# Low parts of the two raw weight quarters by a negative on ScalarE and an adding DMA

## The chip, the cores and the metric

The kernel runs on one core of one Trainium2 chip. The metric is the device time of one execution in microseconds (us), the median of three runs. The core has TensorE (PE), VectorE (DVE), ScalarE (ACT) and GpSimd (POOL), and SyncE (SP) and others issue DMAs. Each engine works through its own instructions in order; semaphores tie them together.

## The reference, cut to what matters

Two transformer blocks run one after the other on 512 tokens of width 1024, all in float32. The part that matters here are products of a token matrix and a weight of 1024 rows: two gates of the first block's mixer and the two feed-forward layers of width 2816.

```python
mix = jax.nn.sigmoid(g_conv) * y_conv + jax.nn.sigmoid(g_attn) * y_attn
h = h + mix @ w_o[l]
n = rmsnorm(h, g_ffn[l])
h = h + (jax.nn.silu(n @ w_gate[l]) * (n @ w_up[l])) @ w_down[l]
```

The second block ends in the same form of feed-forward layer. `g_conv` and `g_attn` are columns of `n @ w_in`.

## The kernel before, in words

A float32 product is made of three products of float32r parts: every operand is split into a high part (a rounded copy, by ACT) and a low part (the operand less its high part, by DVE), and `mm3` (lines 325 to 328) adds high*high, high*low and low*high in one PSUM bank. The third of them, line 328, is the first that reads the weight's low part.

Most columns of the two gates and of the gate and up weights go through `winograd` (line 410): two weight columns at a time, one unit, as seven products of quarters in the place of eight. There are 46 units: 8 in the mixer's gates (from 470 to 565 us of the span), 19 in the first feed-forward layer (650 to 830 us) and 19 in the second (1413 to 1600 us). A unit's weight comes in by one load of 1024 KB on SP (line 397) as four quarters 01, 00, 10, 11 in a tile `raw`. `quarters` (line 392) then makes seven operands in four calls of `parts`, and I call the four pairs of tiles A, B, C and D after their order:

- A: the quarters 01 and 00 as they are (`raw[:, :2]`), 24 matmuls;
- B: the sum of 10 and 11, put in the place of 10 by line 402, and 11 itself, 24 matmuls;
- C: two differences that POOL makes (lines 404 and 405), 24 matmuls;
- D: one difference that DVE makes (line 401), 12 matmuls.

A product of quarters has 4 pairs of tiles times three matmuls of 256 columns, so a unit is 84 matmuls. Each of A to D takes a tile `wh` and a tile `wl`, and there are three buffers of each. So A of the next unit takes the buffers of B of this unit, and D takes those of A: a cast can begin only when PE has read the older tile to its end.

The order of instructions on each engine is fixed when the program is built: a scheduler places them by its own estimate of when each can start. The mixer's gates have more work on POOL and DVE between the units: the sigmoid on ACT, the product with it on POOL (line 651, two to a unit), a sum and a split on DVE.

Of the kernel before, what the change touches and what calls it, by code (L numbers as in the profile page):

```python
# [10 lines left out]
F32 = mybir.dt.float32  # L11
# [3 lines left out]
AF = mybir.ActivationFunctionType  # L15
ALU = mybir.AluOpType
# [10 lines left out]
# wo units begun before the last k-tiles of mix are there  # L27
EARLY = 3
# convolution units emitted after each attention head
FILL = [1, 0, 0, 0, 0, 0, 0, 1, 0, 0, 0, 1, 2, 2, 2, 2]  # L30
# the hidden units by the plain product (tile, part); the others by winograd()
# [9 lines left out]
def cut12(x):  # L41
    """x in parts of 12 bits and a rest."""
    out = []
    for _ in range(3):
        e = 2.0 ** (math.floor(math.log2(x)) - 11)
        out.append(math.floor(x / e) * e)
        x -= out[-1]
    return out + [x]


class Stream:
    """Weights as units of [128, n]; the program's order of loads sets their order in memory."""
# [12 lines left out]
    def quarters(self, name, w):  # L65
        """Two columns of tiles by quarters, [row of the product, half of the sum]: 01, 00, 10, 11."""
        k = w.shape[0] // P
        t = w.reshape(2, k // 2, P, 2, P).transpose(2, 3, 0, 1, 4)
        self.add(name, np.stack([t[:, i, j] for i, j in ((0, 1), (0, 0), (1, 0), (1, 1))], 1))
# [32 lines left out]
def layout(i):  # L102
    """The program's inputs: permuted, tiled and joined copies of the arrays."""
# [78 lines left out]
    # rows of the outputs by the latent attention, the recurrence and the memory  # L182
# [23 lines left out]
    t = np.arange(P)  # L206
# [19 lines left out]
class Ring:  # L226
    """Slots that tiles of one role take in turn."""
# [14 lines left out]
class Kernel:  # L242
# [87 lines left out]
    def lin(self, w, x, out=None, first=True, last=True, k0=0):  # L330
        """out[m, t] += sum over k of w[k, m] x[k, t], w a loaded unit."""
        if out is None:
            out = self.ps("mm", 3)
        k = w[0].shape[1]
        for j in range(k):
            self.mm3(out, (w[0][:, j], w[1][:, j]), x[k0 + j], first and j == 0, last and j == k - 1)
        return out
# [9 lines left out]
    def parts(self, raw):  # L347
        """Quarters of a weight, [128, q, n], or sums of them, in two parts."""
        q, n = raw.shape[1:]
        w = [self.wp.tile([P, q * n], F32R, tag=t, bufs=3, name=self.name(t)) for t in ("wh", "wl")]  # L350
        w = [a.rearrange("p (q n) -> p q n", q=q) for a in w]
        self.split(*w, raw)
        return [[a[:, j].rearrange("p (k c) -> p k c", c=P) for a in w] for j in range(q)]

    def product(self, out, w, x, part, first=True, last=True):
        """out += w^T x[part], x by pairs of tiles as in halves()."""
        for k, (h, l) in enumerate(x):
            self.mm3(
                out, [a[:, k] for a in w], (h[:, part], l[:, part]), first and k == 0, last and k == len(x) - 1
            )  # L360

    def halves(self, src, rb, gain, out, done=None):
        """The right-hand operand src * gain * rb of winograd(): by pairs of a tile of each half of the sum,
        the parts 00, 10, 11, T1, T2, T3, -T4 of [128, 256] (indices: half of the sum, half of the tokens)."""
# [27 lines left out]
    def quarters(self, name):  # L392
        """A weight by quarters for winograd(): 01, 00, S1, 11, S4, S2, S3 as operands."""
# [6 lines left out]
        w = self.parts(raw[:, :2])  # L400
# [9 lines left out]
    def winograd(self, w, x, out):  # L410
        """A product of [2 tiles, 512] by seven products of quarters for eight (Winograd's form of Strassen's).
        out: the two rows of tiles, [128, 512] in SBUF."""
# [4 lines left out]
        # (00, 01) and (10, 11) of the result  # L417
# [21 lines left out]
    def bank(self):  # L439
        """A PSUM bank in two halves, the six of the tags in turn."""  # L440
        self.banks += 1
        ps = self.ps(*(("mm", 3), ("S", 2), ("mm", 3), ("S", 2), ("mm", 3), ("o", 1))[self.banks % 6])
        return ps.rearrange("p (a b) -> p a b", a=2)

    def operand(self, n, k, big=True):
        """Tiles for the two parts of a [k * 128, 512] matrix: list of (high, low)."""
# [13 lines left out]
    def square_sum(self, acc, src, first, scale=1.0, last=False):  # L460
        """acc += (src * scale)^2"""
# [10 lines left out]
    def sums(self, accs):  # L472
        """Sums over the partitions, tokens on the partitions: [128, tokens / 128] in PSUM."""
# [11 lines left out]
    def rstd(self, sums, dim, pre=None, post=1.0):  # L485
        """pre / sqrt(pre^2 sums / dim + eps) * post; shapes [128, ...] alike."""
# [15 lines left out]
        # a first value within 4% by the bits as an integer, then Newton's steps  # L502
# [10 lines left out]
    def bcast(self, r):  # L513
        """A per-token column, [128, n], as rows on every partition: [128, n * 128] in SBUF."""
# [8 lines left out]
    def start(self):  # L523
        """The first operand, and three units by row along with it."""
# [27 lines left out]
    def block1(self):  # L552
# [110 lines left out]
        # the operand's last tiles come late: the first products begin with the others  # L663
# [38 lines left out]
    def keys_steps(self, g, n, rb):  # L702
        """Keys of group g and queries of its four heads; the last step yields them."""
# [25 lines left out]
    def conv(self, n, rb, out):  # L729
        """The short convolution's gated outputs, one unit a step."""  # L730
# [21 lines left out]
    def nsa_cmp(self, g, qg, kc, kcz, gbr):  # L752
        """The compressed branch's weights for four heads, by key: rows 32 hh + key."""
        nc = self.nc
        mm = nc.tensor.matmul
        # scores by key, each head's keys in rows of their own, then by query
# [39 lines left out]
    def nsa_soft(self, h, q, kg, gbr):  # L796
        """The two causal branches' weights of a head, by query, times their gates."""
# [30 lines left out]
    def nsa_out(self, h, pt, pc, vc, V, o32):  # L828
        """The weights by key: transposed, split, then times the values."""
# [28 lines left out]
    def blocks(self, n, rb, first, out):  # L858
        """Overlapping blocks of keys and values: [128 = (half, feature), 16 places, 4 heads x 32 blocks]."""
# [22 lines left out]
    def compress(self, blocks):  # L882
        """Hidden units of the compressed keys and values in four steps, then the products into (kc, vc)."""
# [23 lines left out]
        # the values' hidden units four times over  # L907
# [14 lines left out]
        # values: rows 32 hh + block, zero but for the head hh of a group  # L922
# [15 lines left out]
    def ffn(self, pre, x, gain, n, nhold, acc, done, half=None):  # L938
        """w_down^T (silu(y w_gate) * (y w_up)), y = x * gain normed; n: x * gain as an operand; acc: its
        squares' sums; done(t, sum) takes each finished tile."""  # L940
# [53 lines left out]
        # the hidden units as an operand; the first four take the weights' tiles  # L994
# [25 lines left out]
    def tables(self):  # L1020
        """Rotation by position, times the gains: out = x * one + swapped x * two."""
# [6 lines left out]
        # five [128, 4, 32] temporaries  # L1028
# [42 lines left out]
    def rotate(self, out, x, one, two, tmp):  # L1071
        """x, one, two: [128, n, 64]; out [128, n, 2, 64], twice the same."""
# [10 lines left out]
    def hgrn(self, n, rb, rt, fill):  # L1083
        """Gated linear recurrence, as one causal [512, 512] matrix per head.

        A pair (s, t), s < t, belongs to the level m (a power of two) at which s lies in the lower and t
        in the upper half of one block of 2 m tokens; its decay is the product of the gates after s in
        the lower half (B) and of those up to t in the upper half (A)."""
        nc, c = self.nc, self.c
        # the gates' lower bound: a softmax over two rows of logits  # L1090
# [25 lines left out]
        # by head: k times B, then q times A  # L1116
# [5 lines left out]
        def diagonal(h):  # L1122
            """The pairs s == t."""
# [32 lines left out]
    def hgrn_level(self, m, h, z, fs, last=False):  # L1156
        """One level's factors, split: k times B of the lower halves and q times A of the upper; then the
        next level's, by the halves' total decays."""
# [5 lines left out]
        if not last:  # L1164
            # a block's total is at its first token
# [53 lines left out]
    def mem_operand(self):  # L1219
        """The memory as an operand without its per-token scale; the sum of its squares."""  # L1220
# [13 lines left out]
    def mem_kv(self, ops, hold, r, rb, kk, vv):  # L1234
        """The memory's keys and values, unit by unit."""
# [33 lines left out]
    def mem_soft(self, h, q, f, kk):  # L1269
        """A head's weights by query; f: the queries' scale, [128, 4]."""  # L1270
# [39 lines left out]
    def mla_kv(self, ckv, rt, sckv, krs, kn, kp, vh, vl):  # L1310
        """Keys and values by token; the keys normed but for the gain, their rotary part twice. Two steps
        of products and four of norms."""
# [21 lines left out]
        # the shared rotary part  # L1334
# [8 lines left out]
        # (sckv k_nope, rt k_rope) over their joint norm  # L1343
# [24 lines left out]
    def mla_q(self, cq, scq):  # L1368
        """Queries by token, a block of tokens a step, and their scale."""
# [28 lines left out]
    def mla_turn(self, h, qn, qp, kn, kp, gain):  # L1398
        """A head's queries and keys by feature."""
# [68 lines left out]
    def attended(self, po, y, gain, acc, h):  # L1468
        """A head's output as an operand, times the gain, and its squares."""
        self.split_gain(*y, po, gain[:, h : h + 1])  # L1470
        self.square_sum(acc, po, h == 0, last=h == 3)

    def outs(self, name, y, done):
        """The output's part by the rows of y, two tiles a step."""
# [7 lines left out]
    def block2(self, x, n, nhold, rt, mkv, memkv, final):  # L1482
        """x: the block's input; n: its operand, still without the per-token scale rt."""
# [34 lines left out]
        # sums of squares: of the memory's queries, of the recurrence's outputs, of the low ranks  # L1518
# [35 lines left out]
        def outnorm(j):  # L1554
            """The recurrence's outputs of two heads, normed and gated, as an operand in the place of both."""
# [17 lines left out]
        def scaled(rb, engine=nc.gpsimd):  # L1573
            """Adds an output's part times its per-token scale."""
# [169 lines left out]
```

## Time and profile before

| | us |
|---|---|
| median of three runs | 1743.21 (1736.99 to 1745.76) |
| span of the profiled execution | 1737.1 |
| PE busy in it | 1650.1 (95%) |
| DVE busy | 1263.9 (73%) |
| ACT busy | 834.8 (48%) |
| POOL busy | 562.2 (32%) |

The profile is read from the whole to the part: the engines' shares first, then the same shares for the stages of seven products alone, then who waits for whom there, then one unit instruction by instruction.

### The profile page before, as it was taken

To read this page: it belongs to the slowest core of one execution; us is meant where nothing else is said; L and a number is where in the kernel's file an instruction comes from. 1 tells how busy PE (TensorE), PEld (TensorE's weight loads), DVE (VectorE), ACT (ScalarE), POOL (GpSimd) and SP (SyncE) were. 2 spreads that over 40 slices of the span, in tenths; PEclk is the share of its full clock that TensorE was granted. 3 is DMA by queue.
4 is the path that set the end of the run, shared out by engine and by line. 5 is a ranking of instruction groups with operands and counts; after the bars stand their busy time and mean duration, and the time that the engine had idled before them with its cause. 6 is when DMAs were issued, how large, how long until landed. Compare 5 with 4: busy or idle time off the path is not lost.

```text
span 1737.1 us, 25869 instructions
## 1 busy us (share of the span) xinstructions
PE 1650.1 (95%) x9952; PEld 1454.7 (84%) x9952; DVE 1263.9 (73%) x2157; ACT 834.8 (48%) x1447; POOL 562.2 (32%) x517
## 2 busy tenths in 40 slices
PE   7888899999998999999999999999899989999999
PEld 6776777777898879999888998988778779999887
DVE  6777777768299689999943645875786899999622
ACT  5365666654354444554643433353764444455311
POOL 0224334464055354333121005631513263333000
PEclk9899999999999999999999999999999999999999
DMA  5241001112321522332332332112112303222431
GB/s 162 73 138 37 25 25 37 43 55 93 114 97 54 185 85 98 111 109 98 99 117 90 127 98 85 38 37 64 37 49 73 109 25 121 98 98 74 136 118 61
DMA packets 39005, 147.51 MB, mean 85 GB/s; under 512 B 4448, under 2 KB 7008, under 8 KB 32992
## 3 DMA queue, kind: packets, MB, share of 16 engines
q1 hardware_dynamic: 37296, 143.42, 25.0%
q10 hardware_dynamic: 1584, 2.43, 0.4%
q8 instruction: 78, 1.28, 0.3%
q14 instruction: 47, 0.39, 0.1%
HBM read 143.74 MB, written 2.10 MB: 84 GB/s over the span
## 4 chain that ended last, share of the span: by engine, by line
PE 68%; DVE 16%; POOL 5%; ACT 4%; issue 4%; DMA 3%; SPq 0%; ACTq 0%; POOLq 0%; DVEq 0%
PE mm L327 15%; PE mm L326 15%; PE mm L328 15%; PE S L328 3%; PE S L326 3%; PE S L327 3%; DMA raw<-in_ws_dram 2%; PE o L327 2%; PE o L326 2%; PE o L328 2%; DVE wl L320 2%; DVE wl L341 1%; ACT wh L319 1%; PE T L843 1%; DVE xp L341 1%
## 5 line engine op out<-in xcount | busy, mean ns | idle before, releaser
L319 ACT CAST wh<-raw 128x1024 fp32r<-128x1024 f32 (+5 forms) x179 | 176.9, 989 | 335.8 <-PE mm L327 240.0
L320 DVE TENSOR_TENSOR wl<-raw,wh 128x1024 fp32r<-128x1024 f32 (+4 forms) x149 | 177.2, 1191 | 165.1 <-ACT wh L319 163.7
L404 POOL TENSOR_TENSOR d<-raw 128x512 f32<-128x512 f32 x46 | 87.1, 1893 | 309.3 <-ACT wh L340 138.7
L328 PE MATMUL mm<-xp,wl 128*128 128x256 f32 x552 | 157.1, 285 | 5.2 <-DVE wl L341 5.2
L326 PE MATMUL mm<-xp,wh 128*128 128x256 f32 x552 | 156.6, 284 | 0.0
L327 PE MATMUL mm<-xp,wh 128*128 128x256 f32 x552 | 156.4, 283 | 0.0
L341 DVE TENSOR_TENSOR wl<-raw,wh 128x1024 fp32r<-128x1024 f32 x92 | 141.7, 1540 | 14.9 <-ACT wh L340 14.8
L328 PE MATMUL S<-xp,wl 128*128 128x256 f32 x496 | 142.4, 287 | 9.3 <-DVE wl L341 9.3
L340 ACT CAST wh<-raw 128x1024 fp32r<-128x1024 f32 x92 | 96.6, 1050 | 104.2 <-PE S L327 43.4
L327 PE MATMUL S<-xp,wh 128*128 128x256 f32 x496 | 141.8, 286 | 0.0
L326 PE MATMUL S<-xp,wh 128*128 128x256 f32 x496 | 141.7, 286 | 0.0
L340 ACT CAST wh<-d 128x1024 fp32r<-128x1024 f32 x92 | 76.5, 832 | 87.9 <-POOL d L405 57.7
L328 PEld LDWEIGHTS mm<-xp,wl 128*128 128x128 f32 x552 | 106.1, 192 | 6.4 <-DVE wl L341 6.4
L320 POOL TENSOR_TENSOR wl<-raw,wh 128x1024 fp32r<-128x1024 f32 (+1 forms) x30 | 72.8, 2430 | 112.0 <-ACT wh L319 109.0
L326 PEld LDWEIGHTS mm<-xp,wh 128*128 128x128 f32 x552 | 106.5, 193 | 0.0
L327 PEld LDWEIGHTS mm<-xp,wh 128*128 128x128 f32 x552 | 106.4, 193 | 0.0
L328 PEld LDWEIGHTS S<-xp,wl 128*128 128x128 f32 x496 | 96.8, 195 | 10.1 <-DVE wl L341 10.1
L326 PEld LDWEIGHTS S<-xp,wh 128*128 128x128 f32 x496 | 96.6, 195 | 0.1
L327 PEld LDWEIGHTS S<-xp,wh 128*128 128x128 f32 x496 | 96.6, 195 | 0.1
L469 POOL TENSOR_TENSOR acc<-acc,sq 128x512 f32<-128x512 f32 (+1 forms) x38 | 50.5, 1336 | 142.2 <-ACT sq L468 138.5
L341 DVE TENSOR_TENSOR wl<-d,wh 128x1024 fp32r<-128x1024 f32 x92 | 92.9, 1009 | 4.8 <-ACT wh L340 4.8
L825 POOL TENSOR_SCALAR P<-P,sm 128x128 f32<-128x128 f32 (+3 forms) x128 | 69.0, 565 | 76.9 <-ACT th L340 54.6
(585 smaller groups left out, 5306.4 us busy)
## 6 DMA issues: line engine op xcount, KB each, us to landing
raw<-in_ws_dram SPq DMA_DIRECT2D x136, 512.0 KB, 3.5
raw<-in_ws_dram SPq DMA_DIRECT2D x46, 1024.0 KB, 4.8
raw<-in_ws_dram SPq DMA_DIRECT2D x16, 384.0 KB, 3.1
x<-in_xt_dram SPq DMA_DIRECT2D x16, 256.0 KB, 3.7
raw<-in_ws_dram SPq DMA_DIRECT2D x6, 576.0 KB, 3.8
raw<-in_ws_dram SPq DMA_DIRECT2D x4, 560.0 KB, 4.5
raw<-in_ws_dram SPq DMA_DIRECT2D x8, 256.0 KB, 2.8
x<-in_xt_dram ACTq DMA_DIRECT2D x8, 256.0 KB, 3.6
```

The lines of the kernel that those rows point to most:

```text
L319: nc.scalar.copy(wh, raw)
L320: self.wl_engine.tensor_sub(wl, raw, wh.bitcast(F32))
L326: mm(out, a[0], b[0], start=first, stop=False)
L327: mm(out, a[0], b[1], start=False, stop=False)
L328: mm(out, a[1], b[0], start=False, stop=last)
L340: self.nc.scalar.copy(h, src)
L341: self.nc.vector.tensor_sub(l, src, h.bitcast(F32))
L404: nc.gpsimd.tensor_sub(c[:, 1], a10, a00)
L469: (nc.vector if last else nc.gpsimd).tensor_add(acc, acc, t[:, :w])
L825: nc.gpsimd.tensor_scalar(pi, pi, smv[:, i, b : b + 1], 1.0, op0=ALU.mult, op1=ALU.mult)
L843: nc.tensor.transpose(tp[:, at : at + P], pt[b][i][:, j * P : j * P + P], self.ident)
```

## The change

In the first call of `parts` of each unit, the one for A, the low part is no longer a subtraction on DVE. ACT makes the high part as before (now line 355), then writes its negative into the low part's tile (line 356), and a DMA issued from POOL (line 357) adds the raw quarters to what stands there. B, C and D keep the subtraction. The other differences between the two files are comments that were taken out. All lines of the changed file from here on have numbers greater by 7.

```diff
-    def parts(self, raw):
+    def parts(self, raw, by_dma=False):
         q, n = raw.shape[1:]
         w = [self.wp.tile([P, q * n], F32R, tag=t, bufs=3, name=self.name(t)) for t in ("wh", "wl")]
         w = [a.rearrange("p (q n) -> p q n", q=q) for a in w]
-        self.split(*w, raw)
+        if by_dma:
+            h, l = w
+            self.nc.scalar.copy(h, raw)
+            self.nc.scalar.activation(l, h.bitcast(F32), AF.Copy, scale=-1.0)
+            self.nc.gpsimd.dma_start(l, raw, accum_op=ALU.add)
+        else:
+            self.split(*w, raw)
...
-        w = self.parts(raw[:, :2])
+        w = self.parts(raw[:, :2], True)
```

The scheduler places the instructions anew. On POOL, in the middle of the first feed-forward layer, the order before is only the pairs of lines 404 and 405, where `d` is C's tile and the number tells the unit:

```order
L404 TENSOR_TENSOR d_7222<-raw_7220 128x512
L405 TENSOR_TENSOR d_7222<-raw_7220,d_7222 128x512
L404 TENSOR_TENSOR d_7345<-raw_7343 128x512
L405 TENSOR_TENSOR d_7345<-raw_7343,d_7345 128x512
L404 TENSOR_TENSOR d_7468<-raw_7466 128x512
```

After, at the same place, where the pair has become lines 411 and 412:

```order
L411 TENSOR_TENSOR d_7238<-raw_7236 128x512
L412 TENSOR_TENSOR d_7238<-raw_7236,d_7238 128x512
L357 DMA wl_7241<-raw_7236 128x1024
L411 TENSOR_TENSOR d_7362<-raw_7360 128x512
L412 TENSOR_TENSOR d_7362<-raw_7360,d_7362 128x512
L357 DMA wl_7365<-raw_7360 128x1024
```

A unit's adding DMA stands behind the two differences for C of the same unit.

On ACT, the order before at the end of one unit and the beginning of the next (the first cast is A's, then B's, C's and D's):

```order
L340 CAST wh_7347<-raw_7343 128x1024
L340 CAST wh_7353<-raw_7343 128x1024
L340 CAST wh_7359<-d_7345 128x1024
L340 CAST wh_7363<-d_7346 128x512
L423 COPY g_7367<-S_7369 128x512
```

And after:

```order
L355 CAST wh_7364<-raw_7360 128x1024
L356 ACTIVATE wl_7365<-wh_7364 128x1024
L340 CAST wh_7371<-raw_7360 128x1024
L340 CAST wh_7377<-d_7362 128x1024
L340 CAST wh_7381<-d_7363 128x512
```

The negative stands between A's and B's casts.

On PE, the seam between two units before: D's last matmuls, then A in the order of `mm3` (`wh_7101` and `wl_7102` are A's):

```order
L327 MATMUL mm_7081<-xp_6149,wh_6994 128x256
L328 MATMUL mm_7081<-xp_6148,wl_6995 128x256
L326 MATMUL S_7123<-xp_5998,wh_7101 128x256
L327 MATMUL S_7123<-xp_5999,wh_7101 128x256
L328 MATMUL S_7123<-xp_5998,wl_7102 128x256
L326 MATMUL S_7123<-xp_6048,wh_7101 128x256
```

And after (`wh_7116` and `wl_7117` are A's, `wh_7123` and `wl_7124` B's, `wh_7129` is C's):

```order
L328 MATMUL mm_7096<-xp_6156,wl_7010 128x256
L326 MATMUL S_7139<-xp_6006,wh_7116 128x256
L327 MATMUL S_7139<-xp_6007,wh_7116 128x256
L326 MATMUL mm_7165<-xp_6006,wh_7123 128x256
L327 MATMUL mm_7165<-xp_6007,wh_7123 128x256
L326 MATMUL S_7190<-xp_6006,wh_7129 128x256
L328 MATMUL mm_7165<-xp_6006,wl_7124 128x256
L326 MATMUL mm_7165<-xp_6056,wh_7123 128x256
L328 MATMUL S_7139<-xp_6006,wl_7117 128x256
L326 MATMUL S_7139<-xp_6056,wh_7116 128x256
```

Seven matmuls, two of A, four of B and one of C, now stand ahead of the first that reads A's low part; behind that one come the rest of A (21 matmuls), then B's last 20, then C and D. In the feed-forward layers every unit but the first two of each has this form.

## Rows read from the trace of the kernel before

**Rows 1.** The page: busy time, share and instructions of each engine.

```profile
PE 1650.1 (95%) x9952; PEld 1454.7 (84%) x9952; DVE 1263.9 (73%) x2157; ACT 834.8 (48%) x1447; POOL 562.2 (32%) x517
```

**Rows 2.** Stretches: length, busy time (instructions) of each engine, PE's clock, DMA share, GB/s.

```profile
470.00:565.00 95.00, 86.06 (x676) 83.27 (x675) 84.00 (x100) 47.72 (x64) 49.89 (x29) 1.00 0.20 71
660.00:750.00 90.00, 90.00 (x752) 90.00 (x751) 86.41 (x120) 43.08 (x54) 31.50 (x18) 1.00 0.31 108
1510.00:1600.00 90.00, 90.00 (x752) 90.00 (x752) 86.15 (x122) 48.16 (x63) 29.57 (x18) 1.00 0.27 95
```

**Rows 3.** Waits from 655 to 830: who for whom, us, times, longest.

```profile
ACT wh L340 <- PE S L327: 23.6, 14, 1.9
ACT wh L340 <- PE o L327: 14.2, 8, 1.9
```

**Rows 4.** Timeline of one seam: start, length, engine, line, tile [idle before and its end].

```profile
705.87 0.28 PE L328 MATMUL o<-xp,wl 128*128 128x256 f32 x1
...
706.07 0.62 ACT L340 CAST wh<-d 128x512 fp32r<-128x512 f32 x1 [1.75 <-PE o L327]
...
708.75 0.28 PE L328 MATMUL mm<-xp,wl 128*128 128x256 f32 x1
...
708.95 1.05 ACT L340 CAST wh<-raw 128x1024 fp32r<-128x1024 f32 x1 [1.77 <-PE mm L327]
...
710.42 1.22 DVE L341 TENSOR_TENSOR wl<-raw,wh 128x1024 fp32r<-128x1024 f32 x1
...
713.07 0.28 PE L328 MATMUL mm<-xp,wl 128*128 128x256 f32 x1
713.19 0.28 PE L326 MATMUL S<-xp,wh 128*128 128x256 f32 x1
```

**Rows 5.** Groups by line and shape: count, busy us, mean ns, idle time before.

```profile
L341 DVE TENSOR_TENSOR wl<-raw,wh 128x1024 fp32r<-128x1024 f32 x92 | 141.7, 1540 | 14.9 <-ACT wh L340 14.8
L341 DVE TENSOR_TENSOR wl<-d,wh 128x512 fp32r<-128x512 f32 x46 | 37.1, 807 | 0.0
L401 DVE TENSOR_TENSOR d<-raw 128x512 f32<-128x512 f32 x46 | 33.4, 726 | 0.1
L402 DVE TENSOR_TENSOR raw<-raw 128x512 f32<-128x512 f32 x46 | 32.8, 712 | 1.1
L340 ACT CAST wh<-raw 128x1024 fp32r<-128x1024 f32 x92 | 96.6, 1050 | 104.2 <-PE S L327 43.4 <-PE mm L327 26.1 <-PE o L327 19.8
L404 POOL TENSOR_TENSOR d<-raw 128x512 f32<-128x512 f32 x46 | 87.1, 1893 | 309.3 <-ACT wh L340 138.7 <-issue 67.7 <-DVE wl L320 46.1
L405 POOL TENSOR_TENSOR d<-raw,d 128x512 f32<-128x512 f32 x46 | 74.1, 1610 | 3.6
```

**Rows 6.** DMA issues: issuing queue, count, KB each, median us from issue to landing.

```profile
raw<-in_ws_dram SPq DMA_DIRECT2D x136, 512.0 KB, 3.5
raw<-in_ws_dram SPq DMA_DIRECT2D x46, 1024.0 KB, 4.8
```

**Rows 7.** The two long waits of PE, and the slow matmuls behind them (timeline).

```profile
650.90 0.39 PE L328 MATMUL S<-xp,wl 128*128 128x256 f32 x1 [3.23 <-DVE wl L341]
...
652.48 0.42 PE L328 MATMUL S<-xp,wl 128*128 128x256 f32 x1
...
655.74 0.30 PE L327 MATMUL mm<-xp,wh 128*128 128x256 f32 x1
...
1418.08 0.58 PE L328 MATMUL S<-xp,wl 128*128 128x256 f32 x1 [3.81 <-DVE wl L341]
...
1423.79 0.28 PE L327 MATMUL mm<-xp,wh 128*128 128x256 f32 x1
```

**Rows 8.** Stretch of the second slow piece, PE alone: clock and DMA.

```profile
1419.00:1422.00 3.00, 3.00 (x16) 0.50 0.02 5
```

**Rows 9.** The mixer's gates: PE's waits, and two pieces of the chain that ended last.

```profile
PE mm L328 <- DVE wl L341: 5.2, 5, 1.5
PE S L328 <- DVE wl L341: 2.3, 2, 1.5
PE o L328 <- DVE wl L341: 1.5, 1, 1.5
...
502.73 1.78 DVE wl L341
...
526.98 1.80 DVE wl L341
```

## The prediction

> **What bounds the kernel now.** I read the shares of the engines first: PE is busy for 95% of the span, DVE for 73% [rows 1]. That is a mean over unlike stages, so next I read the stretches in which the change acts. In the two feed-forward layers PE is busy for all of 90.00 us and DVE for 86.41 and 86.15 [rows 2]: DVE is nearly full, but PE never waits for it there. 752 matmuls in 90.00 us are 0.12 us each, and a unit of 84 is 10.08 us. So in 38 of the 46 units the bound is PE, and what is taken off DVE buys nothing. Only in the mixer's gates does PE idle (86.06 busy of 95.00), and its waits there are on DVE's subtraction, 5.2 + 2.3 + 1.5 = 9.0 us [rows 9].
>
> The question is then how late a low part can be before PE notices. The waits from 655 to 830 us show that ACT, not PE, does the waiting: its casts wait for the last read of the buffer that they take over [rows 3]. The timeline of one seam gives the slack [rows 4]: the last matmul of B starts at 708.75, A's cast for the next unit at 708.95, DVE's subtraction runs from 710.42 to 711.64, and A's first matmul starts at 713.19, its first read of the low part two matmuls later, at 713.43. So A's low part is there 1.8 us early. ACT has 1.05 us of work in this chain, DVE 1.22.
>
> **The change part by part.** Removed: 46 subtractions on DVE, at 1540 ns [rows 5] 46 x 1.54 = 71 us of DVE. In the feed-forward layers this lies beside PE's matmuls and is worth nothing; in the mixer's gates it can give back at most PE's 9.0 us.
>
> Added on ACT: 46 passes of 128x1024. The nearest row is the cast of the same shape, 1050 ns [rows 5], so 48 us. ACT is busy for about half of these stretches [rows 2], so its room is no concern; the pass's place is. It follows A's cast, which cannot begin before B's buffer is free, and B's cast now stands behind it; B's low part is wanted by the sixth matmul of the new unit and C's high part by the fifth, which the wait for A covers in what follows.
>
> Added on POOL: 46 DMAs of 512 KB, and POOL does its rows in order. A unit's DMA stands behind the two differences for C, 1.89 + 1.61 = 3.50 us [rows 5].
>
> Now the new loop. Let W be the moment at which PE may do the first matmul that reads A's low part. From there the order gives 22 matmuls to A's end (W + 2.64) and 20 more to B's end (W + 5.04). Two chains start from these.
>
> The first is ACT's: the cast starts 0.1 us after B's end (as at 708.95 for a last matmul that starts at 708.75 and takes 0.12 [rows 4]), 1.05, then the negative, 1.05: W + 7.2.
>
> The second is POOL's. D's cast starts 0.1 us after A's end (706.07 against 705.87 + 0.12 [rows 4]) and takes 0.62, DVE's subtraction for D 0.81: W + 4.2. In one half of the units DVE has done lines 401 and 402 of the next unit before that, in the other half it does them behind it, 0.73 + 0.71 more [rows 5]: W + 4.2 or W + 5.6. The two differences for C write where D's source stood, so they start there, and with their 3.50 they end at W + 7.7 or W + 9.1, 8.4 in the mean. This is later than ACT's chain. The DMA is issued at W + 8.4, and with T from issue to landing the next unit's W is at W + 8.4 + T. PE alone would be there at W + 10.08. **The stall of each unit is T - 1.7 us.** Seven matmuls ahead of the wait do not change that, since all 84 of the unit are in the 10.08.
>
> T has no row: this program issues no data DMA from POOL and none that adds. From below, a plain load of 512 KB takes 3.5 us, and one of 1024 KB takes 4.8 [rows 6]. An adding transfer has to read the source and the tile that it adds to, 1024 KB in all, so the 4.8 is the nearer row. From above I take reading, and then reading and writing again, as two transfers of 1024 KB: 9.6 us. Nothing in it can give a gain below zero, since the tile cannot be used before it lands. I take 5.5, a little above the nearer row, because the issue from POOL has no row either; that addition of 0.7 is a choice. The stall is then 3.8 us.
>
> The Trainium skill ("Collectives: The Full Stack", on what the reduce step costs) says that a reducing transfer reads two sources for each write; no run here shows it yet.
>
> A stall of that length costs more than itself. PE waited for 3.23 us before 650.90 and for 3.81 us before 1418.08, and behind each its matmuls ran at about half rate for a while, at a granted clock of 0.50 in the second piece, which is the lower level, 1.2 GHz [rows 7, 8]. From 652.48 to 655.74 there are 15 matmuls in 3.26 us where 15 x 0.12 = 1.80 would do: 1.5 us lost. From 1418.08 to 1423.79 there are 26 in 5.71 in the place of 3.12: 2.6 us lost. The slow matmuls would be those from W on, which stand in the loop. The seven matmuls that are ahead cut the stall's unbroken part, so I take the smaller, 1.5.
>
> Sum for the feed-forward layers: the period goes from 10.08 to 8.4 + 5.5 + 1.5 = 15.4, so 5.3 us for each unit that follows another, 2 x 18 = 36 of them: 191 us. In the mixer's gates two units take 526.98 - 502.73 = 24.25 us now [rows 9], 12.1 each; the same loop would take 15.4, so 3.3 x 7 = 23 us (the 9.0 us of PE's old waits are inside the 12.1). The first units of the three stages I put at nothing: PE waits there for splits of the token matrix too [rows 7], and if the DMA is later than those, it is some 3 us for each. The sum is 214 us. The profiled span is 1737.1, 6 us below the median of 1743.2; made against the span it gives 1951, and I put the difference on the median: **1957 us**.
>
> **The rivals.** First, a short transfer: T between 3.5 and 4.8, with no fall of the clock, since the longest unbroken wait would stay below the 3.23 us that is known to cost something. At 3.5 the period is 11.9, 1.8 x 36 = 65 us, and nothing in the gates, where 11.9 is under 12.1: 1808. At 4.8 it is 13.2, 3.1 x 36 + 1.1 x 7 = 119: 1862. For it speaks that both sides lie on the core; against it that twice the bytes are read.
>
> "DMA: Bandwidth & Descriptors" of the Trainium skill, on the anatomy of one DMA, gives for DMAs issued by GpSimd about 2.0 us and a microsecond for each 436 KB: an estimate by it is 3.2 us for 512 KB, or 1.5 x 36 = 54 us, 1797 in all; for twice the bytes 4.4 us. No row here has such a DMA, and the page's measure is a plain load.
>
> Second, a long transfer: T of 9.6, every stall beyond the 3.81 that cost 2.6. The period is 8.4 + 9.6 + 2.6 = 20.6: 10.5 x 36 + 8.5 x 7 = 438, so 2181 us. It would show if the addition runs far below the rate of a load or if POOL takes long to issue.
>
> Third, on the other side: the transfer is hidden. This decides from T = 1.7 down, or if the differences for C run so early that the DMA is issued 3 us or more before W + 8.4. Then the feed-forward layers stay at 10.08, and the gates give back up to the 9.0 us of waits on DVE: 1734, faster by 0.5%, or no change if only a part comes. Against it stands that no DMA of 512 KB in this trace lands in under twice 1.7 us, and that ACT's own chain is there only at W + 7.2, which leaves 2.9 us at most.
>
> **How the numbers follow.** The forecast, T from 4.8 to 6.5 with a half-rate piece behind each stall, has 0.50; the short transfer 0.18; the long one, anything above 6.5, 0.26; the hidden one 0.06. The likeliest gives 1957. The range takes in both bounds of T: 1805 to 2180. It leaves out the hidden case and the long tail above 9.6. A measurement of this kernel tells about 0.5% from no change. The hidden case splits evenly: faster 0.03, same 0.03; all others are slower, 0.94.
>
> **What would show it.** In the changed profile PE should have, once in each unit, a wait on the DMA of the low part at line 328, some 3 to 4 us long, some 36 times in the feed-forward layers; DVE's share there should fall by a tenth or more and buy nothing; the row of the DMA's issue should show 5 to 6 us; POOL's issue should stand right behind the second difference for C; the clock in these layers should be visibly below 1.00. If PE's clock stays at 1.00, the half-rate term (36 x 1.5 = 54 us) is wrong. If DMA rows show 3.5 us, T is. If PE's wait on the DMA is absent, the loop is wrong: then A's buffer was free sooner than B's end.

## The result and the profile after

The changed kernel takes 1888.16 us in the median of four runs (1884.97 to 1891.69), the kernel before 1740.7 us in four runs beside it (1736.99 to 1745.76). The ratio is 1.0858, with an interval from 1.0823 to 1.0893: slower by 147 us. The profiled span went from 1737.1 to 1883.3 us, 146.2 more. The forecast was 1957 us in a range from 1805 to 2180: the sign and the mechanism hold, the size was 69 us too high.

The page of the kernel after gives busy time, share and instructions of each engine, to be set beside [rows 1]:

```profile
PE 1716.3 (91%) x9952; PEld 1507.7 (80%) x9952; DVE 1168.8 (62%) x2111; ACT 884.8 (47%) x1493; POOL 560.7 (30%) x563
```

DVE lost 95.1 us of work and the kernel became slower. By [rows 5] the 46 subtractions that went are 71 us of this; the 46 of the same shape that stay took 1219 ns each, where the mean of both was 1540. PE has the same 9952 matmuls, yet 66.2 us more busy time: part of them ran slower. The stretches that answer to [rows 2], after (length, busy time and instructions of PE, PEld, DVE, ACT and POOL, PE's clock, DMA share, GB/s):

```profile
470.00:565.00 95.00, 81.88 (x563) 77.54 (x563) 59.21 (x79) 48.84 (x62) 45.14 (x33) 0.91 0.39 106
660.00:750.00 90.00, 75.93 (x515) 73.04 (x514) 50.67 (x80) 37.85 (x45) 25.68 (x22) 0.87 0.38 106
1510.00:1600.00 90.00, 75.88 (x543) 73.03 (x542) 49.27 (x81) 37.20 (x45) 21.16 (x19) 0.91 0.44 123
```

In 90 us of the first feed-forward layer PE does 515 matmuls where it did 752. DVE's share fell from 96% to 56% there and bought nothing. The mean granted clock is 0.87 where it was 1.00.

The waits of PE from 660 to 900 us, after (engine, tile and line, whom it waited for, us in all, times, longest):

```profile
PE S L328 <- DMA wl<-raw: 21.3, 12, 4.3
PE o L328 <- DMA wl<-raw: 8.1, 5, 2.2
PE S L326 <- ACT wh L340: 6.5, 11, 0.6
PE o L326 <- ACT wh L340: 3.0, 5, 0.6
```

Before, PE was never idle in the stretches of [rows 2] in the two layers. Now there is a wait on the adding DMA in each unit, at line 328, where the prediction put it. A second one of 0.6 us, on C's high part, stands ahead of it in nearly every unit. The issues that answer to [rows 6], after (queue, count, KB each, median us from issue to landing):

```profile
raw<-in_ws_dram SPq DMA_DIRECT2D x46, 1024.0 KB, 4.8
wl<-raw POOLq DMA_DIRECT2D x46, 512.0 KB, 4.5
```

The time T that the whole sum hung on is 4.5 us.

Two units, one behind the other, show the loop. First a unit in which PE keeps its clock, from the timeline after (start, length, engine, line, tile, in brackets the idle time before and what ended it):

```profile
749.82 0.85 POOL L357 DMA_DIRECT2D wl<-raw  x1
...
754.40 0.39 PE L328 MATMUL S<-xp,wl 128*128 128x256 f32 x1 [1.69 <-DMA wl<-raw]
...
758.72 1.29 POOL L411 TENSOR_TENSOR d<-raw 128x512 f32<-128x512 f32 x1 [8.04 <-DVE wl L341]
759.67 1.05 ACT L355 CAST wh<-raw 128x1024 fp32r<-128x1024 f32 x1 [1.28 <-issue]
760.08 1.30 POOL L412 TENSOR_TENSOR d<-raw,d 128x512 f32<-128x512 f32 x1
760.75 1.06 ACT L356 ACTIVATE wl<-wh 128x1024 fp32r<-128x1024 f32 x1
762.10 0.87 POOL L357 DMA_DIRECT2D wl<-raw  x1 [0.72 <-ACT wl L356]
```

W is 754.40. POOL's differences end at W + 6.98; the issue waits 0.72 us longer, for ACT's negative, and stands at W + 7.70. The next unit, in which PE's clock falls:

```profile
766.65 0.57 PE L328 MATMUL S<-xp,wl 128*128 128x256 f32 x1 [1.07 <-DMA wl<-raw]
...
773.85 1.29 POOL L411 TENSOR_TENSOR d<-raw 128x512 f32<-128x512 f32 x1 [10.88 <-issue]
775.22 1.30 POOL L412 TENSOR_TENSOR d<-raw,d 128x512 f32<-128x512 f32 x1
776.46 0.85 POOL L357 DMA_DIRECT2D wl<-raw  x1
```

Here W is 766.65, POOL's second difference is the late one, and the issue stands at W + 9.81. These two issues come 12.28 and 14.36 us behind the ones before them. The two kinds take turns. In all the DMA's line waited for ACT's negative 21 times (us, times):

```profile
  ACT wl L356: 17.3, 21
```

Which kind a unit is does not go with the clock: behind W = 807.73, with the clock at 0.50, ACT is the late one (issue at W + 9.15), and behind 877.88, at 1.00, POOL is (W + 8.78). In the units that were read it goes with DVE's order. In the first kind DVE makes lines 408 and 409 of the next unit ahead of its subtraction for D (754.35 and 755.07 against 757.93), in the second kind behind it (772.29 and 773.01 against 771.68). Of PE alone, the 3 us behind W, in five units that follow each other (length, busy time, granted clock, DMA share, GB/s):

```profile
754.30:757.30 3.00, 2.90 (x24) 1.00 0.57 139
766.60:769.60 3.00, 2.95 (x14) 0.52 0.59 191
781.00:784.00 3.00, 2.95 (x24) 1.00 0.59 177
793.20:796.20 3.00, 2.85 (x15) 0.63 0.55 175
807.60:810.60 3.00, 2.87 (x13) 0.51 0.54 164
```

In three of the five PE is at or near the lower level (0.51 to 0.63, with 1.2 GHz at 0.5): 13 to 15 matmuls in place of 24. Read in the same way behind all 46 waits on the DMA, over 2.6 us each, the clock is at 1.00 behind 18 of them and between 0.50 and 0.79 behind 28.

Over the 19 issues of the first feed-forward layer the mean period is (912.26 - 663.88) / 18 = 13.80 us, over the 19 of the second (1742.22 - 1493.71) / 18 = 13.81, and over the gates' eight (572.19 - 475.11) / 7 = 13.87. Against 10.08 and 12.1 before, this makes 3.72 x 18 + 3.73 x 18 + 1.77 x 7 = 146 of the 146 us. The first period of each layer is the longest (15.42 and 16.08); without it the means are 13.70 and 13.67.

### The profile page after: what moved, and what is told of

The parts are those of the page before. It is cut to its first block, busy times and chain, and to the rows that moved or that the text cites. A ratio compares the mean times of both kernels' runs of the same rounds, so it can differ in the third digit from the quotient of the medians.

```text
span 1883.3 us, 26010 instructions
## 1 busy us (share of the span) xinstructions
PE 1716.3 (91%) x9952; PEld 1507.7 (80%) x9952; DVE 1168.8 (62%) x2111; ACT 884.8 (47%) x1493; POOL 560.7 (30%) x563
## 5 line engine op out<-in xcount | busy, mean ns | idle before, releaser
L328 PE MATMUL S<-xp,wl 128*128 128x256 f32 x496 | 159.4, 321 | 53.4 <-DMA wl<-raw 53.4
L411 POOL TENSOR_TENSOR d<-raw 128x512 f32<-128x512 f32 x46 | 59.2, 1288 | 425.6 <-issue 199.5
L326 PE MATMUL S<-xp,wh 128*128 128x256 f32 x496 | 157.6, 318 | 17.1 <-ACT wh L340 17.1
L341 DVE TENSOR_TENSOR wl<-d,wh 128x1024 fp32r<-128x1024 f32 x92 | 87.8, 955 | 125.1 <-ACT wh L340 125.1
L328 PEld LDWEIGHTS S<-xp,wl 128*128 128x128 f32 x496 | 110.8, 223 | 59.7 <-DMA wl<-raw 59.7
L327 PE MATMUL S<-xp,wh 128*128 128x256 f32 x496 | 154.5, 311 | 0.0
L326 PEld LDWEIGHTS S<-xp,wh 128*128 128x128 f32 x496 | 109.7, 221 | 23.2 <-ACT wh L340 23.0
L327 PEld LDWEIGHTS S<-xp,wh 128*128 128x128 f32 x496 | 110.0, 222 | 0.1
L328 PE MATMUL o<-xp,wl 128*128 128x256 f32 x240 | 75.6, 315 | 22.8 <-DMA wl<-raw 22.8
L826 ACT ACTIVATE P<-P,m 128x128 f32<-128x128 f32 (+3 forms) x128 | 71.3, 559 | 32.2 <-DVE m L822 31.5
```

The source lines that it names most:

```text
L326: mm(out, a[0], b[0], start=first, stop=False)
L327: mm(out, a[0], b[1], start=False, stop=False)
L328: mm(out, a[1], b[0], start=False, stop=last)
L341: self.nc.vector.tensor_sub(l, src, h.bitcast(F32))
L411: nc.gpsimd.tensor_sub(c[:, 1], a10, a00)
L826: nc.scalar.activation(pi, pi, AF.Exp, bias=m, scale=-1.0, accum_out=smv[:, i, b : b + 1])
```

## The experiments

Each change is against the kernel after unless said otherwise; each ratio is against the kernel before, run on the same chip. The kernel before moved by up to 4 us between these sets (1736.6 to 1740.7), so a difference to the kernel after, which was run in a set of its own, is good to some 4 us. There were eleven kernels. They were made to tell apart three things: that the loop over A's buffers sets the end (and not, say, more DMA traffic or ACT's extra pass), what T consists of, and what the fall of the clock costs.

**The slack.** If PE takes B's product ahead of A's, B's buffer is free earlier and A's low part is wanted later. The same turn in the kernel before is the control.

```diff
+        p2 = self.bank()
+        self.product(p2[:, 1], s1, x, 3)
+        self.product(p2[:, 0], a11, x, 6)
         p1 = self.bank()
         self.product(p1[:, 1], a01, x, 1)
         self.product(p1[:, 0], a00, x, 0)
         nc.scalar.copy(half(out[0]), p1)
-        p2 = self.bank()
-        self.product(p2[:, 1], s1, x, 3)
-        self.product(p2[:, 0], a11, x, 6)
```

> The changed kernel (1888 us) with one thing turned round: PE takes pair B of each unit ahead of pair A, so the low part that the DMA makes is wanted 24 matmuls (2.9 us) later, and the buffer that A's cast waits for (B's) is free 24 matmuls earlier. The theory of the late low part: the seam's 13.8 us period is a loop of latencies (buffer free, cast, negative or POOL's differences, DMA 4.5 us), so most of the 3.7 us over 10.08 goes; POOL's differences for C still stand ahead of the DMA's issue and may leave up to 1 us: 1740 to 1785 us. The rival that the DMA's rate, its 24 MB beside the loads, or ACT's extra pass sets the time: nothing of these is changed, so 1880 to 1890.

> The kernel before with pair B ahead of A on PE and no DMA: the control for e1 and e2. PE is full in the feed-forward layers, so no change: 1735 to 1750 us. If the turned order by itself is worth something, it shows here and has to be taken off e1 and e2.

Measured: 1772.72 us with the change (1.0195, 1.0175 to 1.0216) and 1767.25 us without (1.0175, 1.0152 to 1.0198). PE's waits of the whole execution, first with the change, then the control:

```profile
PE S L328 <- DVE wl L341: 20.6, 30, 1.4
...
PE o L328 <- DVE wl L341: 9.6, 15, 1.3
```

```profile
PE S L328 <- DVE wl L341: 15.1, 17, 2.9
...
PE o L328 <- DVE wl L341: 6.6, 7, 2.8
```

The DMA lands as late as before (4.6 us), but almost nobody waits for it. What PE now waits for is B's own low part, which it wants first. The turned order costs about 30 us in the control too, where 1735 to 1750 us had been expected; that wait is a part of it, and the rest was not taken apart. Set against the control the change costs 5.5 us, and the two intervals overlap. So neither the DMA's traffic nor ACT's pass makes the 147 us; the missing slack does.

The same with C's two differences on DVE, so that POOL has nothing ahead of the DMA:

> As e1, and the two differences for C are made by DVE and no longer by POOL, so POOL has nothing ahead of the DMA's issue. Late low part: no wait for the DMA is left in the feed-forward layers, period 10.1, 1735 to 1750 us, at or a little under the kernel before (1741). Rate or ACT's pass: 1880 to 1890. If DVE (again near 96% busy there, 1.54 us less and some 1.4 us more in a unit) becomes the bound: 1760 or more, with PE waiting on DVE.

Measured: 1769.99 us (1.0183, 1.0165 to 1.0201), above the 1735 to 1750 that was expected, and 2.7 us above the control, with overlapping intervals. PE waits for DVE's low parts here as it does in e1 and in the control. POOL's differences hardly matter once there is slack.

**POOL's place in the loop.** The kernel after with C's differences on DVE alone:

```diff
-        nc.gpsimd.tensor_sub(c[:, 1], a10, a00)
-        nc.gpsimd.tensor_sub(c[:, 0], a01, c[:, 1])
+        nc.vector.tensor_sub(c[:, 1], a10, a00)
+        nc.vector.tensor_sub(c[:, 0], a01, c[:, 1])
```

> The changed kernel with the differences for C on DVE, order of PE as in the change. The DMA is then issued when ACT's negative is done, some 2.2 us behind B's end; in the changed kernel about half of the units wait for POOL's differences, 0.5 to 1.4 us longer. Late low part: the period falls by about 0.5 us on the mean, 36 to 43 units, 1862 to 1878 us. Rate of the DMA: 1888, unchanged. If POOL's order were all of it: under 1800.

Measured: 1859.53 us (1.0717, 1.0658 to 1.0776), 29 us below the kernel after and a little below the range that was expected. The view of the DMA's line says what POOL stood idle for ahead of it (us, times):

```profile
  ACT wl L356: 411.9, 36
```

ACT's chain is now the late one in 36 units, and it is nearly as long as POOL's was. The prediction had ACT 1.2 us ahead in the mean; here the mean period falls by 0.2 us in the first layer, 0.4 in the second and 1.0 in the gates.

**ACT's pass, without the DMA.** The negative stays, and DVE adds the raw quarters:

```diff
-            self.nc.gpsimd.dma_start(l, raw, accum_op=ALU.add)
+            self.nc.vector.tensor_add(l, l.bitcast(F32), raw)
```

> The changed kernel with ACT's negative kept, but the raw quarters added to it by DVE in the place of the DMA. Late low part: the chain behind B's end is 0.1 + 1.05 + 1.05 on ACT and 1.2 on DVE, 3.4 us, inside the 4.3 us of C and D and the two matmuls of A: 1735 to 1755 us. If ACT's extra pass is the cost: near 1888.

Measured: 1748.82 us in ten runs (1.0062, 1.0043 to 1.0081). The negative alone costs 11 us; the other 136 come with the DMA, its wait and the clock behind it.

**The addition in the DMA.** The same transfer without the addition (the raw quarters then overwrite the negative):

```diff
-            self.nc.gpsimd.dma_start(l, raw, accum_op=ALU.add)
+            self.nc.gpsimd.dma_start(l, raw)
```

> The changed kernel with a plain copy of the raw quarters by the same DMA from POOL, without the addition (the low parts of A are then the raw quarters, so this part of the result is left wrong). It prices the addition: if reading the tile it adds to costs as much again, issue to landing falls from 4.5 to about 3.4 us and the time by 1.1 us for some 40 units, to 1840 to 1855; if the addition is free, 4.5 and 1888 stay.

Measured: 1782.96 us (1.0261, 1.0225 to 1.0297), below all that was expected. Issues of the copy, its DMA queue (packets, MB, share of the 16 engines' span), and PE alone in two stretches:

```profile
wl<-raw POOLq DMA_DIRECT2D x46, 512.0 KB, 2.9
```

```profile
q0 software_dynamic: 6624, 24.12, 3.7%
```

```profile
660.00:750.00 90.00, 83.41 (x666) 1.00 0.40 142
750.00:830.00 80.00, 74.18 (x599) 1.00 0.40 143
```

The copy lands after 2.9 us, so the addition costs 1.6 us of T, 0.3 of which is POOL's own time at the issue (last section). And the clock stays at 1.00 in these two stretches. The mean period, without the first of each layer, is 11.30 and 11.25 us, which is 8.4 + 2.9: the prediction's loop without its half-rate term. But this is a mean of two kinds that take turns, about 10.7 and 11.5 to 12.0 us. PE's waits from 660 to 860 us tell why:

```profile
PE S L326 <- ACT wh L340: 7.1, 12, 0.6
PE o L326 <- ACT wh L340: 2.9, 5, 0.6
PE S L328 <- DMA wl<-raw: 2.6, 4, 1.0
PE o L328 <- DMA wl<-raw: 0.9, 2, 0.6
```

Most of what PE still waits here is the 0.6 us on C's high part, in nearly every unit: PE's new order asks for it at the fifth matmul. 10.08 + 0.6 is the shorter kind, so by this a faster DMA alone would not have taken the period below 10.7. The 102 us between the costs of this run and of the kernel after (45 and 147) are, worked out and not measured apart, 1.6 x 43 = 69 us of addition and, on top, some 33 us of the clock that went with the longer idle time.

In the kernel after, the same queue with the same bytes has

```profile
q0 software_dynamic: 6624, 24.12, 6.7%
```

1.8 times the share. The Trainium skill's statement that a reducing transfer reads two sources for each write ("Collectives: The Full Stack", in the section on the bandwidth ceiling) agrees in direction; the runs show the time, not the reads.

**Half the bytes.** The DMA adds one of the two quarters, DVE the other:

```diff
-            self.nc.gpsimd.dma_start(l, raw, accum_op=ALU.add)
+            self.nc.gpsimd.dma_start(l[:, :1], raw[:, :1], accum_op=ALU.add)
+            self.nc.vector.tensor_add(l[:, 1:], l[:, 1:].bitcast(F32), raw[:, 1:])
```

> The changed kernel with the DMA adding one of A's two quarters (256 KB) and DVE the other. It prices the DMA by size. A fixed cost and a part by bytes: with 4.5 us for 512 KB, issue to landing between 2.9 (fixed part 1.3) and 4.0 us (fixed part 3.5). The shorter DMA alone takes its saving off some 40 units, and POOL's issue stands where it did: 1830 to 1870 us.

Measured in a single run: 1806.28 us, beside 1736.58 for the kernel before. Issues, and PE alone:

```profile
wl<-raw POOLq DMA_DIRECT2D x46, 256.0 KB, 3.3
```

```profile
660.00:750.00 90.00, 77.61 (x598) 0.94 0.37 106
750.00:830.00 80.00, 71.35 (x582) 1.00 0.38 116
```

Halving the bytes takes 1.2 us from T, so if the cost is linear in the bytes, which two sizes cannot show, 512 KB cost 2.4 us by size and some 2.1 us whatever the size. The time came out below what was expected. Two parts of that were not priced apart: the clock, back at 1.00 in the second stretch, and PE's order, in which the scheduler left no matmul of C ahead of the wait, so that the wait on C's high part (25 us in the kernel after) is gone.

**The clock.** Twenty matmuls that nobody reads, behind each unit's last product:

```diff
         self.product(p4[:, 0], s3, x, 5)
+        junk = self.ps(*self.side)
+        for _ in range(20):
+            nc.tensor.matmul(junk[:, :W], x[0][0][:, 0, :P], x[0][0][:, 0], start=True, stop=True)
```

> The changed kernel with 20 matmuls of 256 columns behind each unit whose product nobody reads, 2.4 us of PE work in the place of idling. If the half-rate matmuls behind each wait are a part of the loss (some 1.2 us in a unit), the granted clock in the feed-forward layers goes from about 0.91 back to near 1.00 and the time falls, though PE does more: 1835 to 1870 us. If the clock is no part of it, 1888 at best; if PE has no idle time to spare for it, up to 1888 + 46 x 2.4 = 1998.

Measured: 1856.46 us (1.0688, 1.0653 to 1.0723), 32 us less than the kernel after, with 920 matmuls more. The two stretches (columns as in [rows 2]):

```profile
660.00:750.00 90.00, 83.50 (x655) 81.73 (x655) 54.40 (x86) 38.90 (x46) 26.59 (x22) 0.96 0.43 115
750.00:830.00 80.00, 78.82 (x647) 77.62 (x646) 44.88 (x74) 38.09 (x46) 21.29 (x19) 1.00 0.46 128
```

PE busy in the gap keeps its clock nearly whole, and the period of the first layer falls from 13.80 to 13.07 us. The loop itself, which no filling shortens, leaves the remaining 119 us. The scheduler also moved matmuls from ahead of the wait to behind it (two are left ahead, of seven), which lengthens the loop by an estimated half microsecond (4 matmuls of 0.12), so by this estimate the 32 us are rather a lower bound for the clock's part.

**The gates alone.** The adding DMA only in the eight units of the mixer's gates:

> The change in the mixer's 8 units alone; the 38 units of the feed-forward layers as before. From the two traces: the mixer's period went from 12.1 to about 13.6 us, 7 x 1.5 = 10 us, so 1748 to 1756 us. If the cost were the same for each of the 46 units (147 / 46 = 3.2 us), 1766.

Measured: 1752.5 us (1.0072, 1.0039 to 1.0106), 14.5 us slower. The rest lies in the feed-forward layers.

**More slack, where PE waits for DVE.** PE's order B, C, D, A, with the sums of the results put behind A; and the same order in the kernel before as the control.

> The changed kernel with PE's order in a unit B, C, D, A and the sums of the results behind A. The buffers then come free in the order B, C, D, A, so A's cast for the next unit waits for C of this unit, and A's low part is wanted only behind D, A, B, C and D: some 11 us, against 2.2 us of ACT, the differences and 4.5 us of DMA. B's low part has A's 24 matmuls (2.9 us) from D's end, more than the 2.35 of a cast and a subtraction that it lacked in e1 and e3. Late low part: no PE wait on the DMA nor on DVE in the feed-forward layers, period 10.08, and up to 9 us from the mixer's gates: 1728 to 1745 us. If another cost of the DMA remains (rate, contention with loads, POOL): 1760 or more. The sums at a unit's end and the banks that they hold may cost some us at the stages' ends.

> The same order of PE and of the sums in the kernel before, without the DMA: the control for e9. DVE keeps the subtraction for A and is near 96% busy. If the order itself is free: 1735 to 1745 us; e9 less this is what the change is worth once its low part is in time, between -9 and 0 us by the gates' waits on DVE, and 0 if PE is the only bound.

Measured: 1773.12 us with the DMA (1.019, 1.0162 to 1.0217) and 1803.18 us without (1.0369, 1.0345 to 1.0394). Issues and one stretch with the DMA, then that stretch of the control (columns as in [rows 2]):

```profile
wl<-raw POOLq DMA_DIRECT2D x46, 512.0 KB, 4.6
```

```profile
660.00:750.00 90.00, 87.48 (x714) 85.89 (x713) 59.80 (x96) 48.42 (x59) 32.32 (x27) 1.00 0.51 141
```

```profile
660.00:750.00 90.00, 79.94 (x623) 77.70 (x624) 70.15 (x97) 36.45 (x46) 30.60 (x16) 0.94 0.26 93
```

That the first would beat the kernel before was a miss: no wait on the DMA is left, but this order has waits of its own on low parts made by DVE, in both kernels. The control, expected at 1735 to 1745, was a miss too. Set against it, though, the change makes the kernel 30 us faster. PE's waits on DVE's low parts of the units (line 341) fall from 39.6 us in the control to 20.7, and the clock in this stretch is 1.00 and not 0.94. Where PE's order does wait for DVE's chain, taking a subtraction off DVE pays, with the same 4.6 us of landing. What exactly costs the control 67 us over the kernel before was not taken apart. No kernel of these beats the one before.

## Why the prediction came out as it did

**What bounds, and what DVE is worth.** Right. PE set the pace of the feed-forward layers, DVE's relief there bought nothing, and the same relief did pay in the order where PE waits for DVE.

**The loop.** Right in form: the wait is at line 328, once a unit, on the DMA. In the kernel after the formula gives 8.4 + 4.5 = 12.9, and the measured 13.69 (mean of the two layers, without the first periods) leaves 0.8 for the clock. That the 8.4 holds is in part luck, since its branches were off in ways that nearly cancel: each of POOL's differences took 1.29 and 1.30 us, not the 1.89 and 1.61 of [rows 5], so POOL's chain was 0.9 us shorter; ACT's chain was 0.5 us longer (W + 7.70 against 7.2). So in every second unit ACT ends the loop, which the prediction had excluded, and POOL in the others. At full clock the issues stand at about W + 7.7 and at W + 8.3 to 8.8, at half rate mostly at about W + 9.2 and W + 9.8. The W + 9.81 behind 766.65 is the prediction's W + 5.6, the two differences' 2.6 and 1.6 us of slow matmuls. With T at 2.9 the formula still meets the mean, but there the wait on C's high part sets every second period.

**T.** Mis-sized: 4.5, not 5.5. The 4.8 of the plain load of 1024 KB [rows 6] was the nearer row, as the prediction said, and the 0.7 put on top of it, because the issue from POOL had no row, was the error: 1.0 x 36 + 1.0 x 7 = 43 us of the 69. The Trainium skill's anatomy of one DMA ("DMA: Bandwidth & Descriptors") gave as an estimate 3.2 us for 512 KB and 4.4 for twice that; the traces show 2.9 for the plain copy and 4.5 for the adding one, so its second reading, bytes counted twice, was the one to take.

**The half-rate term.** The price of one fall was right, its frequency was not. Behind 766.65, A's 22 matmuls took 4.25 us in place of 2.64, 1.6 us lost, beside the 1.5 of the forecast. (Its row, from 652.48 to 655.74, holds 14 matmuls and not 15, so 1.6 were lost there too.) But 28 of the 46 units have it, some of them in part, and the loop leaves 0.8 us for it in the mean: 0.7 x 43 = 30 us. Together the two make 73 us, a little more than the whole miss of 69.

**The rivals.** The short transfer was defined by T from 3.5 to 4.8, and T does lie there; but it went on to say that the clock would not fall, since no unbroken wait would reach 3.23 us. It would have given 8.4 + 4.5 = 12.9, 2.8 x 36 + 0.8 x 7 = 107 us, 1850; the measured 1888 lies between it and the forecast. Its condition on the clock was wrong: the clock fell after waits of which the longest unbroken one was 1.07 us. The long and the hidden transfer fell with T.

**The signs.** PE's waits were forecast as 3 to 4 us long; they are 1.1 to 1.8 us on the DMA in 34 of 46 units, with 0.6 us on C's high part ahead of it. That wait the prediction had named and counted as covered. In the kernel after it is, for the sum, and it breaks up the idle time; with the plain copy it is not. POOL's issue was to stand right behind the second difference; in 21 of 46 units it waits for ACT's negative first.

**The gates.** 1.8 us for a unit in place of 3.3, 12 us in all by the trace and 14.5 by the kernel that changes only them; the smaller T and the rarer falls are the same as in the layers.

## What to carry to other kernels

Before taking work off a busy engine, look whether anyone waits for it at that place: here a nearly full DVE was never waited for, and the replacement, which starts only when a buffer comes free, was judged by its latency against 1.8 us of slack and not by the work it took over. Follow such a replacement round its whole loop (buffer free, cast, negative, issue, landing, first read) and compare the loop with the period. When an experiment reorders work to give slack, run the same order without the change as a control: the two orders here cost 30 and 67 us by themselves, which would have hidden that the change was nearly free in one and gained 30 us in the other.

## What the runs showed of the hardware that was not expected

An adding DMA of 512 KB within the core takes 4.5 us from issue to landing where the plain copy takes 2.9, and its issue keeps POOL for 0.87 us where the copy's takes 0.57. These are the DMA's lines on POOL, after and in the copy (instructions, ns of the shortest, the median and the longest, first and last start):

```profile
L357 POOL DMA_DIRECT2D wl<-raw x46: 849/870/1035, 475.1 to 1742.2; - x46
```

```profile
L357 POOL DMA_DIRECT2D wl<-raw x46: 567/570/736, 474.1 to 1644.4; - x46
```

PE's granted clock fell to its lower level after idle time in short pieces (0.58 and 1.07 us within 2.6 us, ahead of 766.65), although with waits of up to 1.5 us in the gates before it read 1.00 over the whole stage [rows 2, 9]. The length of the wait does not order the cases: behind 1.69 us at 754.40 it stayed at 1.00, behind 1.07 us at 766.65 it was at 0.52, and behind 1.69 us again at 807.73 it was at 0.50. Which property of the idle time decides was not settled; filling the gap with matmuls brought it to 0.96 and 1.00 in the two stretches.

POOL's differences on the same tiles took 1.29 us in place of a mean of 1.89 [rows 5], without a change of their own. In the kernel before they come in two kinds. This is the first difference before (ns of the shortest, the median and the longest) and after (busy us, mean ns, and the idle time before it):

```profile
L404 POOL TENSOR_TENSOR d<-raw x46: 1278/2159/2350, 470.0 to 1599.8; 128x512 f32<-128x512 f32 x46
```

```profile
L411 POOL TENSOR_TENSOR d<-raw 128x512 f32<-128x512 f32 x46 | 59.2, 1288 | 425.6 <-issue 199.5
```

Two meetings with DVE's subtraction in the kernel before go both ways:

```profile
690.34 1.22 DVE L341 TENSOR_TENSOR wl<-raw,wh 128x1024 fp32r<-128x1024 f32 x1
690.55 2.16 POOL L404 TENSOR_TENSOR d<-raw 128x512 f32<-128x512 f32 x1 [6.74 <-ACT wh L340]
...
699.69 1.30 POOL L404 TENSOR_TENSOR d<-raw 128x512 f32<-128x512 f32 x1 [5.54 <-issue]
...
700.00 2.07 DVE L341 TENSOR_TENSOR wl<-raw,wh 128x1024 fp32r<-128x1024 f32 x1 [0.44 <-ACT wh L340]
```

In both, the instruction that began second is the long one. In the kernel after, DVE is busy for 56% of the stretch and not 96%, and its subtraction of this shape takes 1.22 us in the mean. That the two engines hold each other up is likely from this, and no run here varied it alone.
